# Seven block products for eight in some pairs of k-tiles of the feed-forward layers

## The chip, the cores and the metric

The kernel runs on one core of a Trainium2 chip. The metric is the device time of one execution in microseconds (us); the lower the better. The engines named below are PE (TensorE, the matrix unit) with its weight loads PEld, DVE (VectorE), ACT (ScalarE), POOL (GpSimd) and SP (SyncE, which issues most transfers).

## The reference

The program is a decoder trunk of two layers on 256 tokens (SEQ) of width 2,048 (D_MODEL). Layer 0 mixes tokens by retention, layer 1 by latent attention (MLA); each mixer is followed by a dense SwiGLU layer with an inner width D_FF of 5,632. All values are float32.

```python
def rms_norm(x, g):
    y = x * lax.rsqrt(jnp.mean(x * x, axis=-1, keepdims=True) + NORM_EPS)
    return y * g

def swiglu(x, w_gu, w_down):
    gate, up = jnp.split(x @ w_gu, [D_FF], axis=-1)
    return (jax.nn.silu(gate) * up) @ w_down

for i in range(DEPTH):
    h = rms_norm(x, norm_mix_pre[i])
    h = retention(h, ...) if i % 2 == 0 else mla(h, ...)
    x = x + rms_norm(h, norm_mix_post[i])
    h = rms_norm(x, norm_ffn_pre[i])
    x = x + rms_norm(swiglu(h, ffn_w_gu[i], ffn_w_down[i]), norm_ffn_post[i])
```

## The kernel before

**Products.** Every product of activations and weights is made in float32 accuracy out of three faster matmuls (type fp32r). Each operand is split into a rounded part `hi` and the rest `lo`, and hi x hi, hi x lo of the weights, and lo of the activations x hi are summed in a PSUM bank. `split` (L194) writes `hi` on ACT and `lo` (source less `hi`) on DVE. A gain of the norm in front, where there is one, is multiplied into the weights in the same two instructions (`gcol`, L200 and L201; without a gain L197 and L198).

**Tiling.** The 256 tokens are two row tiles t of 128. A group (`group`, L218) makes 1,024 output columns: four banks b00, b01, b10, b11 (row tile, column half of 512). It walks over the k-tiles, 128 rows of the weights each: 16 in gate/up, 44 in down. For each k-tile `weights` (L187) has SP load 128x1024 raw weights (512 KB, four buffers `raw`) and splits them into `w_hi` and `w_lo` (five buffers each, WB). `run` (L230) then issues 12 matmuls of 128x512: two row tiles, two column halves, three each. PE does them in the order of the program; row tile 1 runs `lead` k-tiles behind at the start of a group, and in pieces at its end.

**Gate/up.** `swiglu` (L614) runs 11 groups per layer, each 512 gate and 512 up columns. The left side is `hT`, the transposed input, split by `norm_piece` (L290) from a PSUM tile that PE transposed. After a group ACT takes silu of the gate half (`fsg`, L634), DVE multiplies (`fa`, L636), PE transposes (`ftp`, L621) and ACT copies to `aT` (L622).

**Down.** `closing` (L331) runs two groups (`half`) of 1,024 columns over 44 k-tiles, with `aT` as the left side, split two k-tiles at a time into `ah` and `al` (L337), followed by the norm behind the sub-layer, the update of the residual `xs` and, piece by piece, the next input (`next_input`, L319). The same function closes retention and MLA.

**Order.** A scheduler of the framework orders the instructions of each engine ahead of time; within an engine they run in that order. Small jobs (`later`, `step`) are inserted some k-tiles further on. PSUM has eight banks: six `mm` banks for groups and two `misc` banks for transposes and the like.

Of the kernel before, what the change touches and what calls it, by code (L numbers as in the profile page):

```python
# [51 lines left out]
def trunk(  # L52
# [165 lines left out]
    def group(lhs, kts, load, name, lead=2, skew=0, tail=0, banks=None, between=None):  # L218
# [11 lines left out]
        def run(t, kt, w, cs):  # L230
            whi, wlo = w
            for left, right in ((0, whi), (0, wlo), (1, whi)):
                for c in cs:
# [1 line left out]
                    nc.tensor.matmul(  # L235
                        banks[t][c][:, 0:n],
                        lhs(kt, t, c)[left],
                        right[:, a : a + n],
                        start=kt == 0 and left == 0 and right is whi,
                        stop=kt == kts - 1 and left == 1,  # L240
                    )
# [769 lines left out]
```

## Time and profile before

| what | value |
|---|---|
| median of 3 runs | 2494.71 us (2494.21 to 2496.16) |
| the profiled execution: time, span | 2494.0 us, 2492.2 us |
| mean granted TensorE clock | 0.999 of full speed |
| matmuls of 128x512 in gate/up on `w_hi`, on `w_lo` (both layers) | 2816, 1408 |
| loads of raw weights in gate/up, in down | 352, 176 |

The profile page lists instructions by line, engine and operation; "out<-in" gives the program's names of what is written and read, then the shapes, the count (x2816), busy us, the mean ns of one, and the idle time of the engine just before, with the engine and line that ended it. A row of waits reads: who waits, on whom, for how many us in total, how often, and the longest. A row of the timeline or of the chain of waits begins with the start in us from the start of the span and the length in us.

### The profile page before, as it was taken

What the parts mean: (1) busy time and instruction counts of PE and PEld (TensorE: products, weight loads), DVE (VectorE), ACT (ScalarE), POOL (GpSimd) and SP (SyncE); (2) the same over time, 40 slices, a digit from 0 to 9 for tenths busy, and PEclk for the clock granted to TensorE, in tenths of its full rate; (3) what the DMA queues carried; (4) which work ended last, traced back from release to release, by engine and by line L of the source; (5) the groups of instructions that cost most, each with busy time, mean ns of one, the idle gap of its engine ahead of it and who ended that gap; (6) DMA issues with size and microseconds to landing.
All of it is one profiled execution on the core that took longest, in us unless ns stands there. A gap on an engine that the chain in (4) does not pass through costs nothing.

```text
span 2492.2 us, 29758 instructions
## 1 busy us (share of the span) xinstructions
PE 2479.9 (100%) x11308; PEld 2057.1 (83%) x11308; DVE 1437.8 (58%) x1667; ACT 1244.3 (50%) x1535; POOL 22.4 (1%) x38
## 2 busy tenths in 40 slices
PE   9999999999999999999999999999999999999998
PEld 7888888888888888888888888888888888888887
DVE  7655655656656554454556576875654545445655
ACT  5444445445546444444445465654644444444543
POOL 0000000000000000000000000000000000000000
PEclk9999999999999999999999999999999999999999
DMA  7555555555655555555555665445565555655664
GB/s 249 195 187 179 177 184 182 178 182 185 201 188 193 188 193 186 191 188 189 192 190 197 197 192 156 129 131 195 185 194 189 185 193 186 193 190 190 194 203 144
DMA packets 129599, 463.69 MB, mean 186 GB/s; under 512 B 14640, under 2 KB 15024, under 8 KB 129456
## 3 DMA queue, kind: packets, MB, share of 16 engines
q1 hardware_dynamic: 129456, 461.80, 57.2%
q8 instruction: 88, 1.44, 0.2%
q14 instruction: 55, 0.45, 0.1%
HBM read 459.64 MB, written 2.10 MB: 185 GB/s over the span
## 4 chain that ended last, share of the span: by engine, by line
PE 98%; DVE 1%; DMA 1%; ACT 0%; issue 0%; SPq 0%; POOL 0%; DVEq 0%; POOLq 0%; ACTq 0%
PE gu_b L235 39%; PE dn_b L235 19%; PE rvg_b L235 14%; PE rto_b L235 7%; PE rqk_b L235 7%; PE mlo_b L235 4%; PE q L235 3%; PE mc_b L235 1%; PE ftp L621 1%; PE ry L568 1%; PE htp L294 0%; PE asc L853 0%; PE rsc L523 0%; PE asc L850 0%; PE ztp L586 0%; PE rtp L513 0%
## 5 line engine op out<-in xcount | busy, mean ns | idle before, releaser
L235 PE MATMUL gu_b<-gu_w_hi,hT 128*128 128x512 f32 x2816 | 768.0, 391 | 0.0
L201 DVE SCALAR_TENSOR_TENSOR gu_w_lo<-gu_w_raw,gcol,gu_w_hi 128x1024 fp32r<-128x1024 f32 x352 | 451.9, 1285 | 464.1 <-ACT gu_w_hi L200 462.6
L200 ACT ACTIVATE gu_w_hi<-gu_w_raw,gcol 128x1024 fp32r<-128x1024 f32 x352 | 404.8, 1151 | 481.4 <-PE gu_b L235 478.1
L235 PEld LDWEIGHTS gu_b<-gu_w_hi,hT 128*128 128x128 f32 x2816 | 524.5, 188 | 106.9 <-ACT hT L197 0.3
L235 PE MATMUL gu_b<-gu_w_lo,hT 128*128 128x512 f32 x1408 | 434.5, 390 | 0.0
L235 PEld LDWEIGHTS gu_b<-gu_w_lo,hT 128*128 128x128 f32 x1408 | 264.1, 188 | 55.8 <-DVE gu_w_lo L201 0.6
L198 DVE TENSOR_TENSOR dn_w_lo<-dn_w_raw,dn_w_hi 128x1024 fp32r<-128x1024 f32 x176 | 215.7, 1225 | 152.6 <-ACT dn_w_hi L197 152.6
L235 PE MATMUL rvg_b<-rvg_w_hi,hT 128*128 128x512 f32 x1024 | 280.7, 391 | 0.0
L197 ACT CAST dn_w_hi<-dn_w_raw 128x1024 fp32r<-128x1024 f32 x176 | 184.9, 1051 | 149.6 <-PE dn_b L235 136.5
L201 DVE SCALAR_TENSOR_TENSOR rvg_w_lo<-rvg_w_raw,gcol,rvg_w_hi 128x1024 fp32r<-128x1024 f32 x128 | 164.1, 1284 | 153.7 <-ACT rvg_w_hi L200 152.8
L200 ACT ACTIVATE rvg_w_hi<-rvg_w_raw,gcol 128x1024 fp32r<-128x1024 f32 x128 | 147.5, 1152 | 190.0 <-PE rvg_b L235 180.2
L235 PEld LDWEIGHTS rvg_b<-rvg_w_hi,hT 128*128 128x128 f32 x1024 | 191.0, 188 | 38.9
L235 PE MATMUL dn_b<-dn_w_hi,dn_ah 128*128 128x512 f32 x704 | 219.2, 390 | 0.0
L235 PE MATMUL dn_b<-dn_w_lo,dn_ah 128*128 128x512 f32 x704 | 218.7, 389 | 0.0
L235 PE MATMUL dn_b<-dn_w_hi,dn_al 128*128 128x512 f32 x704 | 218.7, 389 | 0.0
L235 PE MATMUL rvg_b<-rvg_w_lo,hT 128*128 128x512 f32 x512 | 158.0, 390 | 0.0
L235 PEld LDWEIGHTS dn_b<-dn_w_lo,dn_ah 128*128 128x128 f32 x704 | 132.2, 188 | 27.5
L235 PEld LDWEIGHTS dn_b<-dn_w_hi,dn_al 128*128 128x128 f32 x704 | 132.2, 188 | 27.4
L235 PEld LDWEIGHTS dn_b<-dn_w_hi,dn_ah 128*128 128x128 f32 x704 | 131.9, 188 | 27.1
L235 PE MATMUL rqk_b<-rqk_w_hi,hT 128*128 128x512 f32 x512 | 141.0, 392 | 1.2 <-ACT rqk_w_hi L200 1.2
L200 ACT ACTIVATE rqk_w_hi<-rqk_w_raw,gcol 128x1024 fp32r<-128x1024 f32 (+1 forms) x65 | 73.8, 1138 | 84.7 <-PE rqk_b L235 75.6
L201 DVE SCALAR_TENSOR_TENSOR rqk_w_lo<-rqk_w_raw,gcol,rqk_w_hi 128x1024 fp32r<-128x1024 f32 (+1 forms) x65 | 81.5, 1266 | 58.6 <-ACT rqk_w_hi L200 58.6
(212 smaller groups left out, 2564.5 us busy)
## 6 DMA issues: line engine op xcount, KB each, us to landing
gu_w_raw<-w_gu SPq DMA_DIRECT2D x352, 512.0 KB, 3.5
dn_w_raw<-w_down SPq DMA_DIRECT2D x176, 512.0 KB, 3.5
rvg_w_raw<-ret_vg SPq DMA_DIRECT2D x128, 512.0 KB, 3.5
rto_w_raw<-ret_out SPq DMA_DIRECT2D x64, 512.0 KB, 3.5
rqk_w_raw<-ret_qk SPq DMA_DIRECT2D x63, 512.0 KB, 4.5
mlo_w_raw<-mla_out SPq DMA_DIRECT2D x32, 512.0 KB, 3.6
uq_w_raw<-mla_up SPq DMA_DIRECT2D x32, 448.0 KB, 3.3
mc_w_raw<-mla_c SPq DMA_DIRECT2D x16, 512.0 KB, 4.4
```

The source lines that it names most:

```text
L197: nc.scalar.copy(out=hi, in_=src)
L198: nc.vector.tensor_sub(out=lo, in0=src, in1=hi.bitcast(F32))
L200: nc.scalar.activation(out=hi, in_=src, func=AF.Copy, scale=g)
L201: nc.vector.scalar_tensor_tensor(out=lo, in0=src, scalar=g, in1=hi.bitcast(F32), op0=ALU.mult, op1=ALU.subtract)
L235: nc.tensor.matmul(banks[t][c][:, 0:n], lhs(kt, t, c)[left], right[:, a : a + n], start=kt == 0 and left == 0 and right is whi, stop=kt == ...
L568: nc.tensor.matmul(y, left, right, start=n == 0, stop=n == len(terms) - 1)
L621: nc.tensor.transpose(tp[:, b * P : (b + 1) * P], a[:, b * P : (b + 1) * P], ident)
```

## The change

It has three parts.

**Seven products for eight.** In gate/up all groups but the first of a layer treat k-tiles 4 and 5, and 8 and 9, as a pair (`GU_SEVENS`, numbers of pairs); in down each half does so with pairs 2, 6, 10, 14 and 18 (k-tiles 4 and 5, 12 and 13, and so on). In a pair the two row tiles and two k-tiles of the left side, and the two k-tiles and two column halves of the weights, make 2 x 2 blocks; Strassen's method in Winograd's form makes their product with seven block products, each of three matmuls. Four sums of left blocks (`left_sums`) are made and split once per pair and used for all groups in gate/up, and for one half in down. Four sums of weight blocks (`right_sums`) are made and split for each pair. Of the pair's first tile only the first column half is split as it is. Products 2, 3 and 4 go straight into b00, b01, b10; 1 and 6 take two more mm banks, 5 and 7 both misc banks, from the first pair of a group to its last. After the last pair (`combine`, `add`) ACT copies product 1, DVE forms three combinations from the four banks, and adds into each of the four running banks in place: into row tile 0's after two more k-tiles of its matmuls, into row tile 1's after four.

**Gains.** The gain of the norm in front is multiplied into the transposed input instead (a DVE multiply in `norm_piece`, 40 times), and the gain of the group norm in four ACT activations instead of one copy per transposed block of retention. The weights are split without gain.

**Buffers.** `tsum` (two tiles of 128x1024 for the sums of weights), `mv` (three of 128x512), `sf` and `sa` for the sums of the left side; the scratch space for dynamic DMA is 2,048 bytes.

```diff
+GU_SEVENS = (2, 4)
+DN_SEVENS = (2, 6, 10, 14, 18)
...
+    def left_sums(a00, a01, a10, a11, sums, hi, lo):
+        nc.vector.tensor_sub(out=sums[:, 0], in0=a10, in1=a11)
+        nc.vector.tensor_sub(out=sums[:, 1], in0=sums[:, 0], in1=a00)
+        nc.vector.tensor_sub(out=sums[:, 2], in0=a00, in1=a10)
+        nc.vector.tensor_add(out=sums[:, 3], in0=sums[:, 1], in1=a01)
+        split(hi, lo, sums)
+
+    def right_sums(raw0, raw1, name):
+        b00, b01 = raw0[:, 0:512], raw0[:, 512:1024]
+        b10, b11 = raw1[:, 0:512], raw1[:, 512:1024]
...
+        nc.vector.tensor_add(out=t1, in0=b00, in1=b01)
+        nc.vector.tensor_add(out=t3, in0=b01, in1=b11)
+        nc.vector.tensor_add(out=t2, in0=t1, in1=b11)
+        nc.vector.tensor_add(out=t4, in0=t2, in1=b10)
+        for both, src, n in ((ta, (1, 3), "a"), (tb, (2, 4), "b")):
+            hi = wp.tile([P, 1024], F32R, tag="whi", bufs=WB, name=f"{name}_t{n}hi")
+            lo = wp.tile([P, 1024], F32R, tag="wlo", bufs=WB, name=f"{name}_t{n}lo")
+            split(hi, lo, both)
...
+            m = {
+                1: (1, lambda: lhs(k0, 0, 0), b(k0, 0)), 2: ((0, 0), lambda: lhs(k1, 0, 0), b(k1, 0)),
+                3: ((0, 1), s[3], b(k1, 1)), 4: ((1, 0), lambda: lhs(k1, 1, 0), t[4]),
+                5: (5, s[0], t[1]), 6: (6, s[1], t[2]), 7: (7, s[2], t[3]),
+            }
+            for i in (1, 6, 5, 7, 2, 3, 4) if final else (1, 2, 3, 5, 7, 6, 4):
+                product(*m[i])
...
+            m1, u, v = kept(0), kept(1), kept(2)
+            nc.scalar.copy(out=m1, in_=ms[1])
+            nc.vector.tensor_add(out=u, in0=ms[6], in1=m1)
+            nc.vector.tensor_add(out=v, in0=ms[7], in1=u)
+            nc.vector.tensor_sub(out=u, in0=ms[5], in1=u)
...
+        def add(t, c):
+            m1, u, v = parts["m1"], parts["u"], parts["v"]
+            if (t, c) == (1, 1):
+                nc.vector.tensor_sub(out=v, in0=ms[5], in1=v)
+            src = {(0, 0): m1, (0, 1): u, (1, 0): v, (1, 1): v}[t, c]
+            nc.vector.tensor_tensor(out=banks[t][c], in0=banks[t][c], in1=src, op=ALU.add)
...
+            if kt == after + 1:
+                adds(0)
+            if kt == after + 3:
+                adds(1)
+            pairs = after <= kt < after + 4 and kt % 2 == after % 2
+            if last or lead <= kt + 1 < kts - max(skew - 1, 0) and not pairs:
                 runs(1, held[1], last and skew > 1)
...
-        split(
-            hT[:, ks, 0, t, :], hT[:, ks, 1, t, :],
-            tp[:, 0 : n * P].rearrange("p (j q) -> p j q", j=n),
-        )
+        part = wp.tile([P, 512], F32, tag="mv", bufs=3, name=f"hx{t}{i}")
+        part = part[:, 0 : n * P].rearrange("p (j q) -> p j q", j=n)
+        nc.vector.tensor_tensor(
+            out=part, in0=tp[:, 0 : n * P].rearrange("p (j q) -> p j q", j=n),
+            in1=gcol[:, col + k0 : col + k0 + n][:, :, None].to_broadcast([P, n, P]), op=ALU.mult,
         )
+        split(hT[:, ks, 0, t, :], hT[:, ks, 1, t, :], part)
...
-                        nc.scalar.copy(
-                            out=yT[:, h * 4 : h * 4 + 4, t, :], in_=tp.rearrange("p (j q) -> p j q", j=4)
-                        )
+                        for j in range(4):
+                            nc.scalar.activation(
+                                out=yT[:, h * 4 + j, t, :], in_=tp[:, j * P : (j + 1) * P], func=AF.Copy,
+                                scale=gain(G_GN, h * 4 + j),
+                            )
```

In the changed program the matmuls of all groups stand at line 398, the splits at 201 (ACT) and 202 (DVE), the sums of weights at 244 to 247, the combinations at 335 to 337 and 343, and the adds at 345. In the excerpts below `gu0_6` is layer 0's seventh gate/up group, `w5` its k-tile 5, `w2_ta` and `w2_tb` the sums of weights of pair 2 (`talo`, `tblo`: their `lo`), and `w4_ta` those of pair 4.

First place: DVE's order around the first pair of a group. Before, and then after:

```order
L201 SCALAR_TENSOR_TENSOR gu0_6_w3_lo_7854<-gu0_6_w3_raw_7851,gcol_74,gu0_6_w3_hi_7853 128x1024
L636 SCALAR_TENSOR_TENSOR fa_7775<-gu0_5_b01_7470,rto_x0_r_6114,fsg_7773 128x512
L636 SCALAR_TENSOR_TENSOR fa_7779<-gu0_5_b11_7472,rto_x1_r_6139,fsg_7777 128x512
L201 SCALAR_TENSOR_TENSOR gu0_6_w4_lo_7872<-gu0_6_w4_raw_7869,gcol_74,gu0_6_w4_hi_7871 128x1024
L201 SCALAR_TENSOR_TENSOR gu0_6_w5_lo_7890<-gu0_6_w5_raw_7887,gcol_74,gu0_6_w5_hi_7889 128x1024
L201 SCALAR_TENSOR_TENSOR gu0_6_w6_lo_7908<-gu0_6_w6_raw_7905,gcol_74,gu0_6_w6_hi_7907 128x1024
```

```order
L202 TENSOR_TENSOR gu0_6_w4_lo_8171<-gu0_6_w4_raw_8168,gu0_6_w4_hi_8170 128x512
L246 TENSOR_TENSOR gu0_6_w2_tb_8181<-gu0_6_w2_ta_8180,gu0_6_w5_raw_8174 128x512
L247 TENSOR_TENSOR gu0_6_w2_tb_8181<-gu0_6_w2_tb_8181,gu0_6_w5_raw_8174 128x512
L202 TENSOR_TENSOR gu0_6_w5_lo_8177<-gu0_6_w5_raw_8174,gu0_6_w5_hi_8176 128x1024
L202 TENSOR_TENSOR gu0_6_w2_talo_8187<-gu0_6_w2_ta_8180,gu0_6_w2_tahi_8186 128x1024
L244 TENSOR_TENSOR gu0_6_w4_ta_8267<-gu0_6_w8_raw_8255 128x512
L245 TENSOR_TENSOR gu0_6_w4_ta_8267<-gu0_6_w8_raw_8255,gu0_6_w9_raw_8261 128x512
L202 TENSOR_TENSOR gu0_6_w2_tblo_8191<-gu0_6_w2_tb_8181,gu0_6_w2_tbhi_8190 128x1024
L246 TENSOR_TENSOR gu0_6_w4_tb_8268<-gu0_6_w4_ta_8267,gu0_6_w9_raw_8261 128x512
L247 TENSOR_TENSOR gu0_6_w4_tb_8268<-gu0_6_w4_tb_8268,gu0_6_w9_raw_8261 128x512
L202 TENSOR_TENSOR gu0_6_w6_lo_8222<-gu0_6_w6_raw_8219,gu0_6_w6_hi_8221 128x1024
```

Where one split per k-tile stood, the sums and their splits now stand, and the sums of the next pair (from raw tiles 8 and 9) stand between the two splits of this one.

Second place: PE, four k-tiles after the last pair of that group (k-tiles 12 to 14, row tile 1). Before, and then after:

```order
L235 MATMUL gu0_6_b00_7781<-gu0_6_w12_hi_8015,hT_87 128x512
L235 MATMUL gu0_6_b01_7782<-gu0_6_w12_hi_8015,hT_87 128x512
L235 MATMUL gu0_6_b10_7783<-gu0_6_w12_hi_8015,hT_87 128x512
L235 MATMUL gu0_6_b11_7784<-gu0_6_w12_hi_8015,hT_87 128x512
L235 MATMUL gu0_6_b10_7783<-gu0_6_w12_lo_8016,hT_87 128x512
L235 MATMUL gu0_6_b11_7784<-gu0_6_w12_lo_8016,hT_87 128x512
```

```order
L398 MATMUL gu0_6_b10_8082<-gu0_6_w13_lo_8362,hT_90 128x512
L398 MATMUL gu0_6_b10_8082<-gu0_6_w13_hi_8361,hT_90 128x512
L398 MATMUL gu0_6_b00_8080<-gu0_6_w14_hi_8388,hT_90 128x512
L398 MATMUL gu0_6_b01_8081<-gu0_6_w14_hi_8388,hT_90 128x512
L398 MATMUL gu0_6_b11_8083<-gu0_6_w12_hi_8349,hT_90 128x512
L398 MATMUL gu0_6_b11_8083<-gu0_6_w12_lo_8350,hT_90 128x512
```

Row tile 1's matmuls of k-tiles 12 and 13 now come bank by bank, six into b10 and six into b11, with the first two of k-tile 14 between them.

Third place: DVE at the same place of the program. Before, and then after (`mv1`, `mv2`: the combinations u and v; `m5`, `m7`: the misc banks):

```order
L201 SCALAR_TENSOR_TENSOR gu0_6_w12_lo_8016<-gu0_6_w12_raw_8013,gcol_74,gu0_6_w12_hi_8015 128x1024
L201 SCALAR_TENSOR_TENSOR gu0_6_w13_lo_8034<-gu0_6_w13_raw_8031,gcol_74,gu0_6_w13_hi_8033 128x1024
L201 SCALAR_TENSOR_TENSOR gu0_6_w14_lo_8052<-gu0_6_w14_raw_8049,gcol_74,gu0_6_w14_hi_8051 128x1024
L201 SCALAR_TENSOR_TENSOR gu0_6_w15_lo_8070<-gu0_6_w15_raw_8067,gcol_74,gu0_6_w15_hi_8069 128x1024
L201 SCALAR_TENSOR_TENSOR gu0_7_w0_lo_8100<-gu0_7_w0_raw_8097,gcol_74,gu0_7_w0_hi_8099 128x1024
```

```order
L336 TENSOR_TENSOR gu0_6_mv2_8304<-gu0_6_m7_8197,gu0_6_mv1_8303 128x512
L202 TENSOR_TENSOR gu0_6_w12_lo_8350<-gu0_6_w12_raw_8347,gu0_6_w12_hi_8349 128x1024
L337 TENSOR_TENSOR gu0_6_mv1_8303<-gu0_6_m5_8196,gu0_6_mv1_8303 128x512
L202 TENSOR_TENSOR gu0_6_w13_lo_8362<-gu0_6_w13_raw_8359,gu0_6_w13_hi_8361 128x1024
L345 TENSOR_TENSOR gu0_6_b00_8080<-gu0_6_b00_8080,gu0_6_mv0_8302 128x512
L345 TENSOR_TENSOR gu0_6_b01_8081<-gu0_6_b01_8081,gu0_6_mv1_8303 128x512
L202 TENSOR_TENSOR gu0_6_w14_lo_8389<-gu0_6_w14_raw_8386,gu0_6_w14_hi_8388 128x1024
L345 TENSOR_TENSOR gu0_6_b10_8082<-gu0_6_b10_8082,gu0_6_mv2_8304 128x512
L202 TENSOR_TENSOR gu0_6_w15_lo_8407<-gu0_6_w15_raw_8404,gu0_6_w15_hi_8406 128x1024
L343 TENSOR_TENSOR gu0_6_mv2_8304<-gu0_6_m5_8196,gu0_6_mv2_8304 128x512
L202 TENSOR_TENSOR gu0_7_w0_lo_8437<-gu0_7_w0_raw_8434,gu0_7_w0_hi_8436 128x1024
L345 TENSOR_TENSOR gu0_6_b11_8083<-gu0_6_b11_8083,gu0_6_mv2_8304 128x512
```

Between the splits stand now the combinations and the four adds in place; two splits, one of them for the next group's first tile, stand between the add into b10 and the add into b11.

More of the change, by code (lines that the diff above doesn't have):

```diff
@@ L228, in group, with product, run @@
             banks = banks[0]
-        def run(t, kt, w, cs):
-            whi, wlo = w
-            for left, right in ((0, whi), (0, wlo), (1, whi)):
+        w = {}
+        plan = []
+        ms = {}
+        def product(bank, a, b):
+            for i, j in ((0, 0), (0, 1), (1, 0)):
+                plan.append(("mm", bank, lambda a=a, i=i: a()[i], lambda b=b, j=j: b()[j]))
+        def run(t, kt, cs):
+            for i, j in ((0, 0), (0, 1), (1, 0)):
                 for c in cs:
                     a, n = cols[c]
[L235 to L240, printed above, removed]
-                    )
+                    plan.append((
+                        "mm", (t, c), lambda kt=kt, c=c, i=i: lhs(kt, t, c)[i],
+                        lambda kt=kt, a=a, n=n, j=j: w[kt][j][:, a : a + n],
+                    ))
         def runs(t, some, by_bank):
@@ new lines, in load_one, with sums, m_banks, seven @@
+        def load_one(kt):
+            step()
+            w[kt] = load(kt, True) if kt % 2 == 0 and kt // 2 in sevens else load(kt)
+        def sums(p):
+            w["t", p] = right_sums(w[2 * p][2], w[2 * p + 1][2], f"{name}_w{p}")
+        def m_banks():
+            for i, bank in ((1, mm_bank), (6, mm_bank), (5, misc_bank), (7, misc_bank)):
+                ms[i] = bank(f"{name}_m{i}")
+        def seven(p, final):
+            k0, k1 = 2 * p, 2 * p + 1
+            def b(kt, c):
+                return lambda: tuple(x[:, c * 512 : (c + 1) * 512] for x in w[kt][:2])
+            s = [lambda i=i: tuple(x[:, i] for x in left(p)) for i in range(4)]
+            t = {i: (lambda i=i: w["t", p][i]) for i in range(1, 5)}
+            m = {
[5 more added lines that the diff above has]
+                product(*m[i])
@@ L254, in group, with adds @@
+        def adds(t):
+            for c in range(2):
+                plan.append(("add", (t, c), lambda c=c: add(t, c)))
+        sevens = sorted(sevens)
+        after = 2 * sevens[-1] + 2 if sevens else kts
         held = [[], []]
         for kt in range(kts):
-            step()
-            w = load(kt)
+            plan.append(("do", lambda kt=kt: load_one(kt)))
+            if kt // 2 in sevens:
+                if kt % 2:
+                    p = kt // 2
+                    plan.append(("do", lambda p=p: sums(p)))
+                    if p == sevens[0]:
+                        plan.append(("do", m_banks))
+                    seven(p, p == sevens[-1])
+                    if p == sevens[-1]:
+                        plan.append(("do", combine))
+                continue
@@ L420, in closing @@
                 lhs, kts, load, f"{name}{half}", skew=skew if half else 0, tail=2 if half else 0,
-                between=first_done if half else None,
+                between=first_done if half else None, sevens=sevens,
+                left=lambda p, half=half: parts["s", half, p],
             )
@@ L624, in transposes, with sums, seen @@
                 )
+            ins = {}
+            held = {}
+            def sums():
+                return (
+                    fp.tile([P, 4, P], F32, tag="sf", bufs=2, name=f"sf{i}"),
+                    fp.tile([P, 4, P], F32R, tag="sa", bufs=4, name=f"sh{i}"),
+                    fp.tile([P, 4, P], F32R, tag="sa", bufs=4, name=f"sl{i}"),
+                )
+            def seen(t, k0, n, part):
+                for p in GU_SEVENS:
+                    if k0 <= 2 * p < k0 + n:
+                        held[t, p] = part[:, 2 * p - k0], part[:, 2 * p - k0 + 1]
+                        if (1 - t, p) in held:
+                            f, hi, lo = sums()
+                            left_sums(*held[0, p], *held[1, p], f, hi, lo)
+                            ins[p] = hi, lo
+            watch[0] = seen
             for j in range(FF // 512):
```

126 lines of the change are left out of this document (89 added, 37 removed).

## The prediction

> **What bounds the kernel now.** I read the profile page first: span, busy shares, granted clock, chain of waits.
>
> ```profile
> span 2492.2 us, 29758 instructions
> PE 2479.9 (100%) x11308; PEld 2057.1 (83%) x11308; DVE 1437.8 (58%) x1667; ACT 1244.3 (50%) x1535; POOL 22.4 (1%) x38
> PEclk9999999999999999999999999999999999999999
> PE 98%; DVE 1%; DMA 1%; ACT 0%; issue 0%; SPq 0%; POOL 0%; DVEq 0%; POOLq 0%; ACTq 0%
> PE gu_b L235 39%; PE dn_b L235 19%; PE rvg_b L235 14%; PE rto_b L235 7%; PE rqk_b L235 7%; PE mlo_b L235 4%; PE q L235 3%; PE mc_b L235 1%; PE ftp L621 1%; PE ry L568 1%; PE htp L294 0%; PE asc L853 0%; PE rsc L523 0%; PE asc L850 0%; PE ztp L586 0%; PE rtp L513 0%
> ```
>
> TensorE (PE) is busy throughout at full clock, makes 98% of the chain that ends last, and the feed-forward products (gu_b, dn_b) are 58% of it. Busy is not yet bound, so the waits come next: who waits for whom.
>
> ```profile
> ACT gu_w_hi L200 <- PE gu_b L235: 478.1, 315, 2.6
> DVE gu_w_lo L201 <- ACT gu_w_hi L200: 462.6, 316, 2.4
> ...
> PE rqk_b L235 <- ACT rqk_w_hi L200: 1.2, 2, 0.9
> PE mc_b L235 <- ACT hT L197: 0.4, 1, 0.4
> ```
>
> ScalarE (ACT) waits for PE to free a weight buffer, VectorE (DVE) waits for ACT, and PE waits for nobody but for a few tenths at the start and at one boundary. So a matmul taken out is worth its place in PE's stream, and DVE has room until that order turns round.
>
> What one place is worth I take from the chain of waits, a stretch of a gate/up group (start, length, count), and then from the timeline of the last down tile:
>
> ```profile
> 852.17 40.84 PE gu_b L235 x180
> ```
>
> ```profile
> 2475.94 0.39 PE L235 MATMUL dn_b<-dn_w_hi,dn_ah 128*128 128x512 f32 x1
> 2475.95 0.19 PEld L235 LDWEIGHTS dn_b<-dn_w_lo,dn_ah 128*128 128x128 f32 x1
> ...
> 2477.98 0.39 PE L235 MATMUL dn_b<-dn_w_hi,dn_ah 128*128 128x512 f32 x1
> ```
>
> 180 matmuls in 40.84 us are **0.2268 us** each (one alone shows 0.39 because they overlap). There the column halves alternate between banks; in the second view all products go to one bank, as they do in the new pairs, and nine intervals from 2475.94 to 2477.98 are 0.2267 us. So the new bank pattern costs nothing.
>
> **The change, part by part.**
>
> **1. Matmuls removed.** A pair of k-tiles took 2 x 12 matmuls and takes 7 x 3. There are 2 layers x 10 groups x 2 = 40 pairs in gate/up and 2 x 2 x 5 = 20 in down, so 180 matmuls go: 180 x 0.2268 = **-40.8 us**. The lower bound of one matmul's price is its weight load, 0.19 (second row of that view), if loads rather than streams set the pace: -34.
>
> The Trainium skill, "TensorE: Matmul & The Clock Gate", section "Back-to-back issue gap", gives about 131 ns per matmul for a sustained stream of loads and 512-column matmuls, and about 216 ns for an isolated one. The trace differs: 227 ns in a stream of 180. By the page's figure the saving would be 180 x 0.131 = 23.6 us and the time 2475; the measured spacing stands.
>
> **2. DVE work added.** The rows for its prices, by form, and for a gate/up group as it was:
>
> ```profile
> L201 DVE SCALAR_TENSOR_TENSOR gu_w_lo<-gu_w_raw,gcol,gu_w_hi 128x1024 fp32r<-128x1024 f32 x352 | 451.9, 1285 | 464.1 <-ACT gu_w_hi L200 462.6
> L198 DVE TENSOR_TENSOR dn_w_lo<-dn_w_raw,dn_w_hi 128x1024 fp32r<-128x1024 f32 x176 | 215.7, 1225 | 152.6 <-ACT dn_w_hi L197 152.6
> L198 DVE TENSOR_TENSOR dn_al<-aT,dn_ah 128x512 fp32r<-128x512 f32 x88 | 60.7, 691 | 47.6 <-ACT dn_ah L197 47.6
> L636 DVE SCALAR_TENSOR_TENSOR fa<-gu_b,rto_x_r,fsg 128x512 f32<-128x512 f32 x22 | 16.5, 748 | 1.1 <-ACT fsg L634 0.2
> L404 DVE TENSOR_TENSOR yg<-dn_b,dn_gp 128x512 f32<-128x512 f32 x16 | 10.7, 682 | 0.0
> L198 DVE TENSOR_TENSOR hT<-htp,hT 128x256 fp32r<-128x256 f32 x16 | 6.1, 416 | 5.6 <-ACT hT L197 5.6
> L660 DVE TENSOR_TENSOR qra<-q,tabqc 128x128 f32<-128x128 f32 x16 | 4.6, 287 | 1.0 <-ACT qn L810 0.8
> 852.17:896.64 44.47, 44.47 (x202) 36.84 (x201) 22.57 (x19) 21.25 (x22) 0.00 (x0) 1.00 0.60 189
> ```
>
> A gate/up group had 22.57 us of DVE work in 44.47. Now it has 14 whole splits and 2 half ones without gain (14 x 1.225 + 2 x 0.69 = 18.5), per pair four sums and two splits of sums (4 x 0.69 + 2 x 1.225 = 5.2, twice), eight combining or adding steps on the banks (8 x 0.68 = 5.4, priced by yg, which reads a bank too) and two fa (1.5): **35.9 us in 44.47 - 6 x 0.2268 = 43.1**, 83%. In down, eight k-tiles with one pair hold 7 x 1.225 + 0.69 + 4 x 0.691 (dn_al) + 4 x 0.287 + 0.69 (sums of the left side) + 5.2 = 19.0 us in 93 matmuls (8 x 12 - 3), 21.1 us, so 90%. On the average DVE keeps up; what matters is where a late DVE result stands in front of PE.
>
> Consecutive DVE instructions overlap, which the timeline shows:
>
> ```profile
> 1364.67 0.68 DVE L198 TENSOR_TENSOR dn_al<-aT,dn_ah 128x512 fp32r<-128x512 f32 x1
> 1365.27 0.68 DVE L404 TENSOR_TENSOR yg<-dn_b,dn_gp 128x512 f32<-128x512 f32 x1
> 1365.87 1.22 DVE L198 TENSOR_TENSOR dn_w_lo<-dn_w_raw,dn_w_hi 128x1024 fp32r<-128x1024 f32 x1
> 1367.00 0.68 DVE L404 TENSOR_TENSOR yg<-dn_b,dn_gp 128x512 f32<-128x512 f32 x1
> ```
>
> Start to start: 0.60 for 512 columns, 1.13 for 1,024.
>
> The Trainium skill, "VectorE: DVE Perf Modes", section "The DRAIN you can't avoid", says that the next DVE instruction starts only when the pipe is empty, and adds that one which is not held starts earlier. Here the next starts 0.08 before the end of the last (0.60 against 0.68), so the trace shows the second case; the first is rival A below.
>
> **3. The pair itself.** It needs six DVE steps and their splits: 0.60 + 1.13 for its two tiles, 4 x 0.60 for the sums, 2 x 1.13 for their splits, 6.4 us, in the 21 x 0.2268 = 4.76 us that PE takes for it. The difference comes out of the lead that DVE has before the pair (the two rows of waits above: 462.6 / 316 = 1.5 us of idle time per tile, with ACT held up by full buffers). I put the exposed part at **0**; the other end is rival B. Refilling after a pair has cover too: its raw tiles are given back after the first sums and a load lands in 3.5 us, while the pair's own two tiles give their buffers back after the first and the third of seven products (first and sixth in a group's last pair).
>
> ```profile
> gu_w_raw<-w_gu SPq DMA_DIRECT2D x352, 512.0 KB, 3.5
> ```
>
> The change also adds a wait here (first excerpt on the change): between the two splits of the first pair's sums DVE's queue holds the first two sums of the next pair, which need raw tile 9, and its buffer is given back by tile 5's split. That split can end at -5.7 on a clock that is zero where PE begins the pair: its buffer was tile 0's, left at -8.16, then 0.2 to ACT, 1.05 for its half, 1.2 for DVE's. The load lands at -2.2, or at -0.6 if it shares the queue with tile 8's (0.60 of 2.72 us, the DMA share of the last window row), two steps later the second split is done at 1.3, and M6 asks for it as the sixth product at 3.4. So a margin of 2 us hides it; behind it wait tile 6's split (needed at 5.2, done at 3.7) and tile 7's.
>
> **4. The seam after a group's last pair**, where the adds into the banks of the running group stand between two matmuls on the same bank (third excerpt on the change: the last add, into b11). Latencies first: PE's result to a reader, and DVE's result to PE's weight load.
>
> ```profile
> 2477.07 0.39 PE L235 MATMUL dn_b<-dn_w_hi,dn_al 128*128 128x512 f32 x1
> ...
> 2477.50 0.60 ACT L120 ACTIVATE junk<-dn_b 128x512 bf16<-128x512 f32 x1 [5.75 <-PE dn_b L235]
> ...
> 6.43 0.75 DVE L201 SCALAR_TENSOR_TENSOR rqk_w_lo<-rqk_w_raw,gcol,rqk_w_hi 128x512 fp32r<-128x512 f32 x1 [0.56 <-ACT rqk_w_hi L200]
> ...
> 7.24 0.19 PEld L235 LDWEIGHTS rqk_b<-rqk_w_lo,hT 128*128 128x128 f32 x1 [0.60 <-DVE rqk_w_lo L201]
> ```
>
> 2477.50 - (2477.07 + 0.227) = 0.20 us from the end of a matmul's place to the reader; 7.24 - (6.43 + 0.75) = 0.06 from DVE to the load. Clock at zero where the last pair begins: PE ends it at 4.76, row tile 0 of the next two k-tiles at 7.48, row tile 1 at 10.21, row tile 0 of two more at 12.93, b10's six at 14.29, two matmuls of tile 14 at 14.74; then comes b11, whose weight load would begin 0.23 earlier, at 14.51. DVE may add into b10 from 10.21 + 0.20 = 10.41; behind it stand, in the order of the third excerpt, a split (from 11.01), the last combination (12.14), a split (12.74) and the add into b11 (13.87), which ends at 14.55; with 0.06 it is 14.61, so PE waits **0.1 us** at each of 20 gate/up seams, 2.4 us by the unrounded 0.12. In down one of the two splits is a 512-column one, the add ends 0.5 earlier and nothing is late. I take **+2.4**. The bounds: 0, and with whole durations end to end and 0.06 at each of five hand-overs 10.41 + 0.68 + 1.225 + 0.69 + 1.225 + 0.69 + 0.30 = 15.22, 0.71 late at all 24 seams, **+17**. No gain is possible, PE's order being fixed.
>
> **5. Gains moved out of the weight splits.** One DVE multiply now stands between the transposes of each new input piece and its cast. At the boundary into the latent projection PE waited for that cast already (0.4, row above): +0.68. At the start the first piece is 256 columns: +0.42. Other boundaries have cover:
>
> ```profile
> 748.97 0.64 ACT L197 CAST hT<-htp 128x256 fp32r<-128x256 f32 x2
> ...
> 751.31 0.61 PE L235 MATMUL gu_b<-gu_w_hi,hT 128*128 128x512 f32 x2
> ```
>
> The cast ends at 749.61, 1.7 us ahead of the first use. So **+1.1**; bounds 0 and 4 x 1.1 = 4.4 if that cover is gone at every boundary. After retention four ACT activations of 128 columns take the place of one copy, 16 times:
>
> ```profile
> L589 ACT COPY yT<-ztp 128x512 f32<-128x512 f32 x16 | 9.1, 566 | 0.0
> L867 ACT ACTIVATE ex<-asc,mx 128x128 f32<-128x128 f32 x16 | 5.9, 371 | 2.9 <-DVE mx L863 2.9
> ```
>
> 4 x 0.37 - 0.57 = 0.9 us more each, 15 us if nothing covered it; ACT is idle half of the span and the result is used many k-tiles later, so nothing. The transfers are the same in number and size.
>
> **The sum.** Against the profiled execution, 2494.0 us (span 2492.2 and 1.8 around it): 2494.0 - 40.8 + 2.4 + 1.1 = 2456.7. The median of the runs is 2494.7, 0.7 above it: **2457.4**.
>
> **Rivals.**
>
> **A. The DVE chain at the seam is longer than I make it.** If instructions that read and write a bank in place don't overlap, or a split waits for its ACT half, each seam costs 0.4 to 0.7 us instead of 0.1: 24 x 0.55 = 13.2 for 2.4, so about **2468**. For it: this in-place add has no row of its own at this size, and DVE is 83 to 90% loaded. Against it: yg reads a bank at 0.60.
>
> **B. The pairs run DVE dry (slower).** Where DVE's lead is gone, each pair takes DVE's 6.4 us instead of PE's 4.76: 60 x 1.64 = 98 us lost for 40.8 gained, 2494.7 + 57.6 = **2552**. It decides from a stall of 0.68 us per pair on. For it: a pair holds four of the five weight buffers, and DVE stands still for tile 9's load; from 2 us of lateness on that reaches PE. Against it: two of them come free early (part 3), and DVE had half its time idle.
>
> **C. A removed matmul is worth only its weight load**, 0.188 us: 33.8 saved, 2494.7 - 33.8 + 3.5 = **2464**. Against it: 0.2268 in every stretch read.
>
> **E. Pairs lose as much as they save**, 0.68 us each, a milder B: **2495**.
>
> **How the numbers follow.** My forecast with its own range of 2453 to 2463 has 0.62, A (2463 to 2475) 0.24, C 0.04, E 0.03, B 0.07. The range takes the bounds of the terms: 2494.7 - 40.8 = 2453.9 without any wait, less the spread of the runs, 2453; and 2453.9 + 17 + 4.4 = 2475. That holds the forecast, A and C, 0.9. A measurement of this kernel tells about 0.2%, 5 us, from no change: faster 0.91, within it 0.02 (two thirds of E; the rest of E is faster), slower 0.07 (B).
>
> **What would show it.** 180 fewer matmuls of 512 columns; a gate/up group of 43.1 to 43.3 us instead of 44.46; DVE near 1,860 us busy (1,438 + 20 x 13.3 + 20 x 6.4 in down + 22 for its seams + 24 for 40 multiplies - 18 for 303 other splits without gain); waits of PE for DVE's add of a few us in all, at the last add of a group. Wrong if PE waits for sums or splits within pairs (B, E), if waits at the adds exceed 5 us (A), or if the spacing in the stretches of whole tiles changes.

## The result, and the profile after

The changed kernel takes 2454.1 us (median of 4 runs, 2453.43 to 2454.15) against 2495.13 us of the kernel before beside it: a ratio of **0.9835** with a 95% interval of 0.9818 to 0.9852, 41 us faster. The forecast was 2457.4. The profiled execution took 2454.15 us with a span of 2452.3.

The page of the changed kernel, with the engines' busy time, the granted clock, and the chain that ended last:

```profile
span 2452.3 us, 30456 instructions
...
PE 2438.9 (99%) x11128; PEld 2023.6 (83%) x11128; DVE 1799.4 (73%) x2379; ACT 1311.1 (53%) x1751; POOL 27.1 (1%) x38
...
PEclk9999999999999999999999999999999999999999
...
PE 99%; DMA 0%; DVE 0%; SPq 0%; ACT 0%; issue 0%; DVEq 0%; POOL 0%; POOLq 0%; ACTq 0%
```

PE lost 180 of 11,308 instructions and 41.0 us of busy time, and is still the whole chain. DVE went from 1437.8 to 1799.4 us. (The prediction's 1,860 added whole durations; the page counts the time in which two DVE instructions overlap once.)

The waits of the changed kernel (who, on whom, us in all, times, longest):

```profile
ACT gu_w_hi L201 <- PE gu_b L398: 252.3, 143, 4.2
DVE gu_w_lo L202 <- ACT gu_w_hi L201: 120.0, 78, 2.5
...
DVE gu_w_ta L245 <- DMA gu_w_raw<-w_gu: 32.2, 24, 1.6
...
PE rqk_b L398 <- ACT hT L201: 1.0, 1, 1.0
```

ACT still waits for PE, but 252 us instead of 478, and DVE for ACT 120 instead of 463: of the first wait, half of the spare time that hid the new work is used up, of the second three quarters. The third row is the wait that the prediction named, DVE standing still for the next pair's raw tile (20 of the 24 times). PE has no row for an add, a sum or a split in the feed-forward layers; the last row is at the very start of the program. A matmul is shown longer (0.39 us) than its place (0.2267), so a short delay of PE leaves no row here; it shows in the starts. Added up over the starts of neighbouring 128x512 matmuls, gate/up has 3.6 us per layer beyond 0.2267 each, and the kernel without any pair (none, below) has 3.6 too.

The chain of waits shows a gate/up group and the part of down with one pair in eight k-tiles as stretches (start, length, count):

```profile
808.37 2.75 PE gu_b L398 x12
...
851.47 2.75 PE gu_b L398 x12
...
1267.34 17.00 PE dn_b L398 x75
...
1288.42 17.00 PE dn_b L398 x75
```

A group now takes 851.47 - 808.37 = 43.10 us for 44.47, which is 1.37 less for six matmuls, 0.228 each; eight k-tiles of down take 21.08, which is 93 x 0.2267. So every removed matmul gave its whole place and nothing was paid in the pairs or at the seams.

### The profile page after: what moved, and what is told of

It reads as the page before. It is cut to its first block, busy times and chain, and to the rows that moved or that the text cites. A ratio compares the mean times of both kernels' runs of the same rounds, so it can differ in the third digit from the quotient of the medians.

```text
span 2452.3 us, 30456 instructions
## 1 busy us (share of the span) xinstructions
PE 2438.9 (99%) x11128; PEld 2023.6 (83%) x11128; DVE 1799.4 (73%) x2379; ACT 1311.1 (53%) x1751; POOL 27.1 (1%) x38
## 4 chain that ended last, share of the span: by engine, by line
PE 99%; DMA 0%; DVE 0%; SPq 0%; ACT 0%; issue 0%; DVEq 0%; POOL 0%; POOLq 0%; ACTq 0%
PE gu_b L398 34%; PE dn_b L398 17%; PE rvg_b L398 14%; PE rto_b L398 7%; PE rqk_b L398 7%; PE gu_m L398 4%; PE mlo_b L398 4%; PE q L398 3%; PE dn_m L398 2%; PE mc_b L398 2%; PE ftp L776 1%; PE ry L721 1%; PE htp L434 1%; PE asc L1032 0%; PE rsc L676 0%; PE asc L1029 0%
## 5 line engine op out<-in xcount | busy, mean ns | idle before, releaser
L398 PE MATMUL gu_b<-gu_w_hi,hT 128*128 128x512 f32 x2256 | 640.8, 392 | 0.0
L201 ACT CAST gu_w_hi<-gu_w_raw 128x1024 fp32r<-128x1024 f32 (+1 forms) x352 | 349.4, 1003 | 327.7 <-PE gu_b L398 252.3
L202 DVE TENSOR_TENSOR gu_w_lo<-gu_w_raw,gu_w_hi 128x1024 fp32r<-128x1024 f32 (+1 forms) x352 | 402.7, 1159 | 120.3 <-ACT gu_w_hi L201 120.0
L398 PEld LDWEIGHTS gu_b<-gu_w_hi,hT 128*128 128x128 f32 x2256 | 419.4, 188 | 85.7 <-DVE hT L202 0.9
L398 PE MATMUL gu_b<-gu_w_lo,hT 128*128 128x512 f32 x1128 | 358.2, 390 | 0.0
L202 DVE TENSOR_TENSOR rvg_w_lo<-rvg_w_raw,rvg_w_hi 128x1024 fp32r<-128x1024 f32 x128 | 156.4, 1224 | 160.6 <-ACT rvg_w_hi L201 160.6
L201 ACT CAST rvg_w_hi<-rvg_w_raw 128x1024 fp32r<-128x1024 f32 x128 | 134.7, 1053 | 195.8 <-PE rvg_b L398 187.4
L201 ACT CAST dn_w_hi<-dn_w_raw 128x1024 fp32r<-128x1024 f32 (+1 forms) x176 | 174.3, 1003 | 104.1 <-PE dn_b L398 55.9
L202 DVE TENSOR_TENSOR dn_w_lo<-dn_w_raw,dn_w_hi 128x1024 fp32r<-128x1024 f32 (+1 forms) x176 | 200.0, 1160 | 23.6 <-ACT dn_w_hi L201 22.9
L202 DVE TENSOR_TENSOR rqk_w_lo<-rqk_w_raw,rqk_w_hi 128x1024 fp32r<-128x1024 f32 (+1 forms) x65 | 77.5, 1207 | 59.3 <-ACT rqk_w_hi L201 59.3
```

The costliest lines, as they stand in the source:

```text
L201: nc.scalar.copy(out=hi, in_=src)
L202: nc.vector.tensor_sub(out=lo, in0=src, in1=hi.bitcast(F32))
L398: nc.tensor.matmul(out, e[2](), e[3](), start=bank not in begun, stop=ends[bank, bank in added] == n, skip_group_check=bank in added,)
```

## The experiments

All times are medians; each ratio is to runs of the kernel before beside it on the same chip.

| kernel | time, us | ratio, 95% interval |
|---|---|---|
| changed kernel | 2454.10 | 0.9835 (0.9818 to 0.9852) |
| none | 2494.51 | 1.0001 (0.9992 to 1.0010) |
| gu_only | 2467.55 | 0.9892 (0.9878 to 0.9906) |
| dn_only | 2481.87 | 0.9949 (0.9937 to 0.9962) |
| before_scratch | 2494.45 | 1.0001 (0.9992 to 1.0010) |
| seam_one | 2455.54 | 0.9841 (0.9827 to 0.9856) |
| seam_two | 2457.69 | 0.9849 (0.9833 to 0.9866) |
| dn_seven | 2453.94 | 0.9838 (0.9823 to 0.9852) |
| dn_nine | 2470.84 | 0.9903 (0.9888 to 0.9917) |
| dn_seven_pool | 2459.11 | 0.9855 (0.9841 to 0.9870) |
| gu_three | 2445.94 | **0.9803** (0.9789 to 0.9818) |
| gu_three_pool | 2451.77 | 0.9828 (0.9812 to 0.9845) |
| both_pool | 2456.08 | 0.9845 (0.9830 to 0.9860) |

Whole times scatter by a microsecond or two at the program's start and end, so the table below has, from each kernel's trace, the length of each feed-forward stage: from the start of its first matmul to that of the next stage's first (in the second layer's down, to its own last). These repeat within 0.2 us where nothing in them was changed. In the last three rows down's first matmuls (two to four) stand ahead of gate/up's last ones, which are 1.4 to 1.5 us of work; there only the sum of the two columns of a layer can be compared with the other rows.

| kernel | gate/up, layer 0 | down, layer 0 | gate/up, layer 1 | down, layer 1 |
|---|---|---|---|---|
| before | 491.83 | 241.39 | 491.91 | 240.08 |
| none | 491.96 | 240.77 | 491.98 | 240.08 |
| changed | 478.39 | 234.54 | 478.38 | 233.28 |
| gu_only | 478.36 | 240.77 | 478.38 | 240.08 |
| dn_only | 491.96 | 234.53 | 491.99 | 233.28 |
| seam_one | 478.62 | 234.84 | 478.59 | 233.28 |
| seam_two | 479.03 | 235.11 | 479.05 | 233.28 |
| dn_seven | 478.37 | 237.25 | 478.39 | 233.27 |
| dn_nine | 478.37 | 241.93 | 478.39 | 239.47 |
| dn_seven_pool | 478.43 | 237.13 | 478.35 | 235.23 |
| gu_three | 472.91 | 235.93 | 472.75 | 234.64 |
| gu_three_pool | 475.23 | 236.48 | 475.23 | 235.23 |
| both_pool | 475.21 | 237.77 | 474.69 | 238.06 |

### Whether the removed matmuls are the gain

**none**

```diff
-GU_SEVENS = (2, 4)
-DN_SEVENS = (2, 6, 10, 14, 18)
+GU_SEVENS = ()
+DN_SEVENS = ()
```

> No pair takes seven products (both lists empty); the moved gains and the new buffers stay. If each removed matmul is worth its whole place of 0.2268 us and the other edits cost about nothing: 2454.1 + 40.8 = 2494.9 us, the time before. If the lighter splits without gain gave part of the gain: 2480 to 2490. If the moved gains cost the 1.1 us that the prediction gave them: 2495.6 to 2496.

It took 2494.51 us, the time before. Together the moved gains, the lighter splits and the new buffers are worth nothing that can be measured (the interval leaves 2 us either way), and the whole gain of 40.4 us (2494.51 - 2454.1) is that of the pairs: 0.224 us for each of 180 matmuls.

**gu_only**

```diff
-DN_SEVENS = (2, 6, 10, 14, 18)
+DN_SEVENS = ()
```

> Seven products in the 40 gate/up pairs alone. If the gain is 120 matmuls by 0.2268 us and the seams cost nothing: 27.2 us under the kernel without any pair, 2467.7. If each gate/up seam loses 0.12 us: 2.4 more, 2470.

It took 2467.55, 27.0 under none. Its gate/up stages are the changed kernel's within 0.03 us, its down stages those of none.

**dn_only**

```diff
-GU_SEVENS = (2, 4)
+GU_SEVENS = ()
```

> Seven products in the 20 down pairs alone. If the gain is 60 matmuls by 0.2268 us: 13.6 us under the kernel without any pair, 2481.3. If pairs in down lose 0.3 us each to DVE at 84% load: 2487.

It took 2481.87, 12.6 under none for the expected 13.6. In the stages the second layer's down is 6.80 us shorter than in none, 30 x 0.2267 exactly, the first layer's 6.24. So the two parts add up (27.0 + 12.6 of 40.4 us), and neither needs the other.

**before_scratch**

```diff
-    nc = bacc.Bacc("TRN2", target_bir_lowering=False, num_devices=1)
+    nc = bacc.Bacc("TRN2", target_bir_lowering=False, num_devices=1, dynamic_dma_scratch_size=2048)
```

> The kernel before with the smaller scratch space for dynamic DMA alone. In the trace after, the stretch from the last matmul to the end is 0.7 us longer than before. If the scratch size does it: 0.7 us over before, 2495.8. If it is the scatter of the last output transfer: no difference in the median, and the ends of single runs 0.6 us apart in both kernels.

2494.45 beside 2494.19, a ratio of 1.0001: the smaller scratch space costs nothing that can be measured. From the last down matmul to the end of the span lie 8.4 us in all profiled kernels but the changed one (9.05), dn_nine (9.4) and both_pool (8.8). In the changed one the last output transfer lands 0.7 us later than elsewhere (7.98 us after the last matmul for 7.3); in dn_nine DVE's last step is 0.96 later already, and in both_pool the time comes after the landing. All profiled kernels but the one before have the small scratch space, so it is not the cause; what the cause is was not followed.

### Why the seam cost nothing

The prediction gave each gate/up seam 0.12 us, and rival A 0.4 to 0.7. The timeline of the changed kernel at such a seam, the pair's first matmul at 1122.90 being zero on its clock:

```profile
1122.90 0.39 PE L398 MATMUL gu_m<-gu_w_hi,hT 128*128 128x512 f32 x1
...
1133.07 0.70 DVE L345 TENSOR_TENSOR gu_b<-gu_b,gu_mv 128x512 f32<-128x512 f32 x1
1133.68 1.22 DVE L202 TENSOR_TENSOR gu_w_lo<-gu_w_raw,gu_w_hi 128x1024 fp32r<-128x1024 f32 x1
1134.81 0.69 DVE L343 TENSOR_TENSOR gu_mv<-gu_m,gu_mv 128x512 f32<-128x512 f32 x1
1135.41 1.22 DVE L202 TENSOR_TENSOR gu_w_lo<-gu_w_raw,gu_w_hi 128x1024 fp32r<-128x1024 f32 x1
1136.54 0.70 DVE L345 TENSOR_TENSOR gu_b<-gu_b,gu_mv 128x512 f32<-128x512 f32 x1
...
1136.95 1.07 PE L398 MATMUL gu_b<-gu_w_hi,hT 128*128 128x512 f32 x4
```

The distances from start to start are those that the prediction took (0.61, 1.13, 0.60, 1.13), in place in a bank too. But the add into b10 starts at 10.17 and not 10.41: of row tile 1's last two matmuls the one into b10 comes first, so b10 is ready one place of 0.23 us earlier. The add into b11 ends at 1137.24. The first matmul into b11 is the fourth of the last row, at 1136.95 + 3 x 0.227 = 1137.63, and its weight load would begin about 0.23 before. So 0.1 us was spare where 0.1 was to be short. Neither condition of rival A holds: the add in place is followed after 0.61, so such instructions overlap, and DVE has no idle time ahead of these splits.

**seam_one**

```diff
             if (t, c) == (1, 1):
-                nc.vector.tensor_sub(out=v, in0=ms[5], in1=v)
+                nc.vector.tensor_tensor(out=u, in0=v, in1=v, op=ALU.max)
+                nc.vector.tensor_sub(out=v, in0=ms[5], in1=u)
```

> One more 128x512 DVE instruction (a maximum of v with itself) in the chain between the add into b10 and the add into b11 of each group's last pair. By the trace after, the add into b11 ends at 14.34 on the seam's clock in gate/up and 14.09 in down's first halves, and the weight load behind it could begin at 14.51; with 0.06 us to hand over, 0.11 and 0.36 us are spare. So with 0.60 us more: 0.49 late at 20 gate/up seams and 0.24 at two of down, +10.3 us, 2464.4. If the seam has room and something else sets the end: 2454. If every added DVE instruction counted in full at all 24 seams: +14.4, 2468.5.

**seam_two**

```diff
             if (t, c) == (1, 1):
-                nc.vector.tensor_sub(out=v, in0=ms[5], in1=v)
+                nc.vector.tensor_tensor(out=u, in0=v, in1=v, op=ALU.max)
+                nc.vector.tensor_tensor(out=m1, in0=u, in1=u, op=ALU.max)
+                nc.vector.tensor_sub(out=v, in0=ms[5], in1=m1)
```

> Two more such instructions in the same chain; the order also puts the last combination right ahead of the add into b11 in gate/up, and one more weight split ahead of it in down. By the spare time of the trace: gate/up 1.20 + 0.15 - 0.11 = 1.24 late at 20 seams, 24.8 us, down 1.20 + 1.13 - 0.36 = 1.97 at two, 3.9 us: +28.7, 2482.8, so that the second instruction costs in full (0.6 us and more per seam), the first less by the spare 0.11. If the seam has room: 2454.

In both, the price that was expected (+10.3 and +28.7) failed, and the time is near the other branch, 2454: +1.4 and +3.6 us in the medians, and in the gate/up stages only 0.2 and 0.7 us for ten seams (478.62 and 479.03 for 478.39). The first layer's down is 0.3 and 0.6 longer; the rest of the medians is not in the feed-forward stages. Yet the add did come later, and PE's weight load did wait for it (seam_two, timeline; here zero is at 1124.47):

```profile
1138.72 0.69 DVE L345 TENSOR_TENSOR gu_mv<-gu_m,gu_mv 128x512 f32<-128x512 f32 x1
...
1139.51 0.70 DVE L347 TENSOR_TENSOR gu_b<-gu_b,gu_mv 128x512 f32<-128x512 f32 x1
...
1140.27 0.19 PEld L400 LDWEIGHTS gu_b<-gu_w_hi,hT 128*128 128x128 f32 x1 [0.19 <-DVE gu_b L347]
```

The add ends at 1140.21 - 1124.47 = 15.74, 1.4 us later than in the changed kernel, and the load starts 0.06 after it, having waited 0.19. What moved is PE's order. This is PE's order at the seam in seam_two (from the last matmul into b10 of k-tile 13 to the first into b11; the names are those of `gu0_6`, the timeline above is of `gu0_8`, whose order is the same):

```
L400 MATMUL gu0_6_b10_8092<-gu0_6_w13_hi_8371,hT_90 128x512
L400 MATMUL gu0_6_b00_8090<-gu0_6_w14_hi_8400,hT_90 128x512
L400 MATMUL gu0_6_b01_8091<-gu0_6_w14_hi_8400,hT_90 128x512
L400 MATMUL gu0_6_b00_8090<-gu0_6_w14_lo_8401,hT_90 128x512
L400 MATMUL gu0_6_b01_8091<-gu0_6_w14_lo_8401,hT_90 128x512
L400 MATMUL gu0_6_b00_8090<-gu0_6_w14_hi_8400,hT_90 128x512
L400 MATMUL gu0_6_b01_8091<-gu0_6_w14_hi_8400,hT_90 128x512
L400 MATMUL gu0_6_b10_8092<-gu0_6_w14_hi_8400,hT_90 128x512
L400 MATMUL gu0_6_b11_8093<-gu0_6_w12_hi_8359,hT_90 128x512
```

Seven matmuls of k-tile 14 stand there between b10 and b11, four in seam_one, two in the changed kernel (the same in every gate/up group, but nine in the last group of a layer of seam_two). The longer the chain was made, the more independent matmuls the scheduler put in ahead of the add's reader. Five more places of 0.227 us are 1.1 us; the add is 1.4 later and 0.1 was spare. The weight load waits 0.19 for what is left, and PE's matmuls come some 0.07 later per seam (0.66 us for ten). So the two matmuls that the prediction counted as a fixed part of PE's order at the seam are best read as such a filling too: the seam's slack is made, not given. Had the seam lain at the end of a group's work, there would be nothing to fill it with; that was not tried.

### How far the pairs can go

**dn_nine**

```diff
-DN_SEVENS = (2, 6, 10, 14, 18)
+DN_SEVENS = (2, 4, 6, 8, 10, 12, 14, 16, 18)
```

> In down every second pair takes seven products (pairs 2, 4, ... 18: nine for five in each half, 16 more pairs in all). If DVE stays hidden: 48 more matmuls less, -10.9 us, 2443. If DVE runs dry (rival B of the prediction): by starts in the trace, eight k-tiles with two pairs need 6 x 1.13 + 2 x 0.60 + 4 x 0.60 + 2 x 1.40 + 2 x 4.66 = 22.5 us of DVE for 90 x 0.2268 = 20.4 us of PE, 2.1 short, 4.5 times in each of four halves: +38 - 10.9 = +27, 2481, less what DVE's lead covers (some us per half).

**dn_seven**

```diff
-DN_SEVENS = (2, 6, 10, 14, 18)
+DN_SEVENS = (2, 5, 8, 10, 13, 16, 18)
```

> In down pairs 2, 5, 8, 10, 13, 16 and 18 take seven products (seven for five in each half, 8 more pairs in all). Six k-tiles with one pair need 14.1 us of DVE for 69 x 0.2268 = 15.6 us of PE, so if only the average load counts: 24 more matmuls less, -5.4 us, 2448.7. If four k-tiles between two pairs (11.25 us of DVE for 10.2 of PE) expose a wait: 2 x 1 us per half given back, 2453 or more.

dn_nine took 2470.84, 16.7 us more than the changed kernel with 48 matmuls fewer; dn_seven 2453.94, no gain for 24 fewer. Busy time in 120 us in the middle of the first layer's down (PE, PEld, DVE, ACT, POOL), for the changed kernel, dn_seven and dn_nine:

```profile
1300.00:1420.00 120.00, 120.00 (x531) 99.39 (x531) 102.03 (x127) 72.97 (x93) 0.00 (x0) 1.00 0.62 202
```

```profile
1300.00:1420.00 120.00, 117.19 (x511) 95.16 (x511) 111.38 (x156) 75.51 (x98) 0.00 (x0) 1.00 0.59 199
```

```profile
1300.00:1420.00 120.00, 115.00 (x493) 91.06 (x491) 118.75 (x173) 75.67 (x101) 0.00 (x0) 1.00 0.59 193
```

DVE goes from 85 to 93 to 99%, and PE from full to 97.7 and 95.8%: at nine pairs DVE has taken PE's place as the bound. With the stage lengths: nine pairs should save 5.44 us per layer on five (24 matmuls), but the first layer's down is longer, so waits cost 241.93 - 234.54 + 5.44 = 12.8 us there and 11.6 in the second: 24.4 for the 38 expected, so that DVE's lead covers a third. Seven pairs save 2.72 per layer and lose 5.4 in the first and 2.7 in the second, by the same reckoning. But the profiled execution of dn_seven took 2456.85 us and the three others 2452.92 to 2454.22, so the 5.4 is more than the usual loss: the median leaves 5.3 for both layers, just what the 24 matmuls save. The waits of PE, first in dn_nine, then in dn_seven:

```profile
PE dn_m L398 <- ACT dn_w_tbhi L201: 13.4, 18, 1.0
```

```profile
PE dn_m L398 <- DVE dn_w_tblo L202: 2.7, 4, 1.1
PE dn_b L398 <- DVE dn_w_lo L202: 2.1, 4, 0.7
```

They are for the splits of the sums of weights and for the splits behind them, the places that the prediction named for its rivals B and E. At 93% it need not be load alone, for DVE also stands still (dn_seven, timeline):

```profile
1386.76 0.69 DVE L245 TENSOR_TENSOR dn_w_ta<-dn_w_raw 128x512 f32<-128x512 f32 x1 [2.18 <-DMA dn_w_raw<-w_down]
```

That is the sum which needs the next raw tile, with a split queued behind it. That this wait, and not the load, is what delays PE is not shown.

**dn_seven_pool**

```diff
-        nc.vector.tensor_add(out=t1, in0=b00, in1=b01)
-        nc.vector.tensor_add(out=t3, in0=b01, in1=b11)
+        nc.gpsimd.tensor_add(out=t1, in0=b00, in1=b01)
+        nc.gpsimd.tensor_add(out=t3, in0=b01, in1=b11)
```

(with dn_seven's list)

> As dn_seven, with the first two sums of weight blocks of every pair (lines 244 and 245, in gate/up too) on POOL. In dn_seven DVE was busy 111.4 of 120 us in the middle of down and stood still up to 2.2 us at line 245 for a load. If DVE's load and that wait are what gave the gain back: 1.2 us of DVE less per pair and no wait in its queue, so the 24 matmuls come out in full, 5.4 us under the changed kernel, 2448.7. If POOL is too slow for it or slows DVE down: 2454 or more.

It took 2459.11, so the second branch came true. POOL needs two to three times DVE's time for such a sum (means of 1.37 to 2.10 us in dn_seven_pool, groups by form), and the DVE sum that runs behind it became slow as well, here in dn_seven_pool and then in the changed kernel:

```profile
L245 POOL TENSOR_TENSOR gu_w_ta<-gu_w_raw 128x512 f32<-128x512 f32 x40 | 67.3, 1683 | 43.6 <-DMA gu_w_raw<-w_gu 43.6
...
L246 DVE TENSOR_TENSOR gu_w_tb<-gu_w_ta,gu_w_raw 128x512 f32<-128x512 f32 x40 | 56.8, 1419 | 4.2 <-DMA gu_w_raw<-w_gu 2.2 <-DVE gu_w_tblo L202 0.9
```

```profile
L246 DVE TENSOR_TENSOR gu_w_tb<-gu_w_ta,gu_w_raw 128x512 f32<-128x512 f32 x40 | 27.5, 687 | 0.5
```

Of the 40 sums in the first of these DVE rows, the five for which POOL stood still took 0.68 us and the 35 for which it was at work 1.53: the two engines hinder each other. Two sums of 0.60 us were taken from DVE and about 0.73 given back in the third; the pair's sums also wait for POOL's slower ones. This run therefore does not part load from waiting in dn_seven; both stay possible there.

**gu_three**

```diff
-GU_SEVENS = (2, 4)
+GU_SEVENS = (2, 3, 5)
...
-                    fp.tile([P, 4, P], F32, tag="sf", bufs=2, name=f"sf{i}"),
-                    fp.tile([P, 4, P], F32R, tag="sa", bufs=4, name=f"sh{i}"),
-                    fp.tile([P, 4, P], F32R, tag="sa", bufs=4, name=f"sl{i}"),
+                    fp.tile([P, 4, P], F32, tag="sf", bufs=1, name=f"sf{i}"),
+                    fp.tile([P, 4, P], F32R, tag="sa", bufs=6, name=f"sh{i}"),
+                    fp.tile([P, 4, P], F32R, tag="sa", bufs=6, name=f"sl{i}"),
...
-                    sg = fp.tile([P, 512], F32, tag="fsg", bufs=2, name="fsg")
+                    sg = fp.tile([P, 512], F32, tag="fsg", bufs=1, name="fsg")
```

> In gate/up pairs 2, 3 and 5 take seven products (20 more pairs; three sets of left sums are kept, one buffer fewer each for sf and fsg makes room). If DVE stays hidden: 60 matmuls less, -13.6 us, 2440.5. DVE would be busy about 38 of 42.4 us in a group, 90%, near dn_seven's 93%, with two pairs in a row (12.8 us of DVE in 9.5 of PE): if its lead of some 3 us does not cover that, 0.3 to 1 us per group is given back, 2447 to 2460.

It took 2445.94, better than both kernels, just below the second branch (2447 to 2460). Gate/up and down together are 4.1 and 4.3 us shorter in the two layers, of the 6.8 that 30 matmuls are worth (the two columns have to be added here: six gate/up matmuls, 1.36 us, come after down's first ones). Down by itself loses nothing: its matmuls have the same distances as in the changed kernel. The loss is in gate/up. Busy time from 800 to 1200 us there, changed kernel first:

```profile
800.00:1200.00 400.00, 400.00 (x1804) 331.45 (x1803) 315.77 (x365) 210.57 (x235) 0.00 (x0) 1.00 0.59 193
```

```profile
800.00:1200.00 400.00, 400.00 (x1794) 328.73 (x1793) 356.61 (x418) 228.78 (x257) 0.00 (x0) 1.00 0.59 195
```

DVE is at 79% and then 89%. PE seems busy throughout in both, but in gu_three its weight loads wait once in each group with pairs (gu_three, waits, and then the chain of waits at the same place of two groups):

```profile
PEld gu_m L398 <- DVE gu_w_tblo L202: 7.6, 20, 0.4
```

```profile
1105.08 2.76 PE gu_b L398 x12
...
1147.76 2.76 PE gu_b L398 x12
```

A group takes 1147.76 - 1105.08 = 42.68 us, where three matmuls fewer than 43.10 would be 42.42: 0.26 us are given back, 5.2 in 20 groups. The wait is in the last pair of a group, for the split of the second sums of weights, which that pair's order asks for as the second product; up to the end of those sums DVE works almost without a gap for 10 us (1114.24 to 1124.38). So at 89% the mechanism of rival E has begun, here behind two pairs in a row; whether the same load costs as much with the pairs apart, or with the `sf` and `fsg` buffers that this kernel gives up, was not tried. In down all of the further saving was lost at 93%.

**gu_three_pool** and **both_pool** have gu_three's edit with dn_seven_pool's two lines, and both_pool has dn_seven's list too.

> As gu_three, with the first two sums of weight blocks of every pair on POOL. If DVE is what holds gu_three back: DVE's work for two pairs in a row falls from 12.8 to 10.4 us, and the time comes to the full 2440.5. If POOL is too slow, or the lead in weight buffers is what runs out: no better than gu_three.

> Three pairs per group in gate/up and seven per half in down, with the first two sums on POOL. If both hold as above: 13.6 + 5.4 under the changed kernel, 2435. Otherwise the losses of the two runs before it add up.

2451.77 and 2456.08: POOL makes gu_three 5.8 us slower, and seven pairs in down a further 4.3. In each, the second branch of what was expected came true. Against the changed kernel gu_three_pool is 2.3 faster and dn_seven_pool 5.0 slower, 2.7 together; both_pool is 2.0 slower, so the losses add up.

## Why the prediction was right, step by step

- **The bound and the price of a matmul.** Right: 180 x 0.2268 = 40.8 forecast, 40.4 between none and the changed kernel, 43.10 us per group of the forecast 43.1. Rival C (0.188 us per matmul) would have made 33.8. The bank pattern cost nothing. DVE was busy 79% in gate/up and 85% in down, for 83 and 90% forecast from whole durations.
- **The pair hidden by DVE's lead.** Right: no wait of PE in any pair, and the same sum of gaps between matmuls as without pairs. DVE did stand still for raw tile 9, up to 1.6 us, and the margin of 2 us held.
- **The seam, +2.4 us.** Mis-sized: it measured 0. The step that failed took the last matmul of row tile 1 for the last into b10, which is one place earlier. Behind that lies a larger mistake of the method: PE's two matmuls between b10 and b11 were taken as given, and seam_one and seam_two show that the scheduler puts in more of them when the chain ahead of the add is longer. Rival A, 13 us, did not occur, and even of 14 and 29 us of added DVE work at the seams only 1.4 and 3.6 were seen.
- **The moved gains, +1.1 us.** Mis-sized: 0 within the interval of none (0.9992 to 1.0010, so up to 2 us either way). At the start, given +0.42, some 0.6 us can be seen, hardly more than the scatter: in the profiles with full clock there, the first matmul of the retention's second weight group (`rvg`) comes at 200.1 to 200.7 us in three with the change and at 199.7 and 200.0 in two without. But the boundary into the latent projection, given +0.68, became shorter: PE's wait of 0.4 there is gone, and the first layer's down with that boundary is 0.62 shorter in none than before. Why the cast came earlier there was not tried.
- **Rivals B and E.** They did not occur, and the mechanism is real: nothing was lost at 79 and 85% of DVE's time, 0.26 us per group at 89%, and at 99% it costs 24 us in down alone. The change was made short of that point.

The two mis-sized terms, 3.5 us, make up the distance of 3.3 from 2457.4 to 2454.1. The time is within 0.2 us of the 2453.9 that the prediction has without any wait: the price of a matmul and the hidden pairs carried the forecast, and the two small terms only moved it away.

## What to carry to other kernels

Where one engine is busy throughout and waits for nobody, work taken off it is worth its full place in the stream, as long as the engine that takes over the work keeps up. In these runs it did so at 79 and 85% of its time; at 89% two fifths of what was added to the saving were lost, at 93% all of it, and at 99% more than it. The share is not the whole measure: where the work comes in a row, or the queue holds an instruction that waits for a load, the loss may begin earlier. A slack read from a schedule is not a constant: with a scheduler that orders instructions ahead of time, a longer chain is partly filled with other work, so price a seam by what is left to fill it with. An idle engine is not free help: POOL was slower at the same sums and slowed the busy DVE down.
